# A two-layer decoder trunk on one core: where x's first pairs lie, when constants and late weights come, and which queue stores the solved triangle

## The chip, the core and the metric

The kernel runs on one core of a Trainium2 chip. The core has a matmul engine (TensorE, here PE, with its weight loads PEld), a vector engine (VectorE, DVE), a scalar engine (ScalarE, ACT), GpSimd (POOL) and SyncE (SP), which mostly issues transfers. SP, ACT and POOL issue DMAs, each in the order of its own queue. The metric is the device time of one execution in microseconds (us); the median of several runs is compared. The profiler records one execution.

## The reference

Two residual layers over 512 tokens of width 2048, all float32. Layer 0 is gated differential attention with 8 heads, layer 1 is RWKV-7 time mixing with 32 heads of 64 channels:

```python
x = x + diff_attention_mixer(rms_norm(x, norm_w[0]), ...)   # 8 heads, q k v gate = h @ w_in
x = x + rwkv7_mixer(rms_norm(x, norm_w[1]), ...)            # 32 heads

# attention, for each head
a = softmax(q1 k1) - lam * softmax(q2 k2)                    # causal
o = rms_norm(a @ v) * silu(gate)                             # then @ w_out

# RWKV, for each head and token t
sa = einsum('bhvk,bhk->bhv', S, a_t)
S = S * w_t + sa * b_t + v_t * k_t
y = einsum('bhvk,bhk->bhv', S, r_t)                          # then group norm, gate, @ w_out
```

## The kernel before, in words

**Products.** Each float32 product is made of three matmuls of rounded parts: a high part (`hH`, `wh`, made by ACT) and a low part (`hL`, `wl`, made by DVE as the difference, L105 and L106). Weights come in pieces of 512 KB into three buffers `wraw`, mostly on SP's queue (L78).

**Order of the queues.** The kernel is traced in Python, and an engine's queue is put in order from the tracing order, priorities (`high_priority(offset)`, with `AHEAD, SCAN, SOLVE = 2000, 3000, 4000`; a higher one goes first among what is expected to be ready) and `issue_after(ins)`, which puts an instruction behind `ins`. Beside the large products run *chains*: generators that are stepped by a count of matmuls. `tick` (L152) counts one matmul for the first chain in the list; a `yield n` in a generator waits for n matmuls. A chain that stands behind another in the list starts to count when that one is through.

**First layer.** `layer0` goes through the heads. Head 0 is made directly (`unit_tok`). Heads 1 to 7 (`unit_head`) use a block scheme in which sums of blocks of x are multiplied by sums of weight blocks: products with the sums S1, S2, S4 and S3 in turn, with products of plain blocks around them. A head has 336 matmuls on which chains are counted. The pairs of rows of x (`pairs`, eight tiles of two rows each) lie in tiles that later have another use: in order V, VL, acc1, G, Ta, Tb, Tc, Td. V and VL later hold a head's values (`head_vg`), acc1 and G the results of its value and gate products and the gate (`gates`, `copy_out`, L248). `input_sums` forms the sums from the pairs; S3, which goes into the places of x's first rows (`hH`, `hL`), is formed in a second call, `late`, once head 0's products have read these. Its high part is one ACT instruction (L491), its low part one on DVE (L492).

While the products of head h run, the attention of head h-1 is worked off as a chain (delay 56 matmuls, in head 1 20). In head 1 the chain `rwkv_consts` stands ahead of it: three DMAs on ACT's queue and some twenty small DVE operations (from L1161 on) that prepare parameters of the second layer, with 10 + 8 matmuls between its steps. In a head, `G` is needed by the products' copies (L248) once the attention of the head before has used its gate (L382); DVE's `take` (L527) then subtracts the product from G and acc1, and `third` writes the next products into the same accumulating bank. The last head works in another order: `square` comes before `third`, which loads its weights itself.

**Second layer.** `layer1` iterates 16 times over pairs of heads. An iteration makes the Gram products (`gram`, L1287, bank gp), stores parts of them on SP (`ltd`, L1301 and L1307), and POOL loads them back as LT. `t_solve` solves a triangular system on DVE in 31 small double steps (L1352, L1354), ends with a product into `Tm` (L1355) and stores it to HBM (`td`, L1356, on POOL's queue, 128 KB). `t_combine`, the first part of the scan's chain in the next iteration, reads it back in another arrangement (`TT`, four DMAs on SP, L1369), transposes two halves on DVE (L1378), waits `GAP_D` = 18 matmuls, makes the products `px` (L1384), and goes on after `GAP_X` = 19 and `GAP_T` = 8 more. Just behind px stand the next Gram products on PE, which need `AR` (L1271), formed on DVE from `mixr` (L1129). SP's queue holds, beside `td`'s readback, the loads of the weights.

Of the kernel before, what the change touches and what calls it, by code (L numbers as in the profile page):

```python
# [38 lines left out]
AHEAD, SCAN, SOLVE = 2000, 3000, 4000  # L39
# [423 lines left out]
NH4 = 8  # L463
# [3 lines left out]
def input_sums(g, pairs, late):  # L467


    nc, w = g.nc, g.work  # L470
    if not late:
        def parts(*tags):

            out, tags = [], list(tags)
            while tags:
                t = tags.pop(0)
                if t[:2] == "dd":
                    at = [g.const.tile([P, 2, 256], F32R, name="sum" + n, tag=n, bufs=1) for n in (t, tags.pop(0))]
                else:
                    at = w.tile([P, 2, 4, 256], F32R, name=t, tag=t, bufs=1)  # L480
                    at = [at[:, 0], at[:, 1]]
                out += [(at[0][:, k], at[1][:, k]) for k in range(at[0].shape[1])]
            return out

        g.sums = {"S1": parts("sA", "sA2"), "S2": parts("sB", "sB2"),
                  "S4": parts("dd0H", "dd0L", "dd1H", "dd1L", "sC2"),
                  "S3": [(g.hH[k][:, 256:512], g.hL[k][:, 256:512]) for k in range(NH4)]}

    def put(nm, k, o, scale=1.0):
        hi, lo = g.sums[nm][k]  # L490
        nc.scalar.activation(hi, o, AF.Copy, scale=scale)  # L491
        nc.vector.scalar_tensor_tensor(lo, o, scale, hi.bitcast(F32), ALU.mult, ALU.subtract)  # L492

    def mixed(o, x, scale, op):

        nc.vector.scalar_tensor_tensor(o, x, scale, o, ALU.mult, op)

    norm = lambda i: g.prm_a[:, i : i + 1]
    if not late:
        minus = g.const.tile([P, NH4], F32, name="minus")  # L500
        nc.vector.tensor_scalar(minus[:], g.prm_a[:, 0:NH4], -1.0, None, ALU.mult)
    for k in range(NH4):
        (a, b), (c, d) = [(pairs[k][:, i, 0:256], pairs[k][:, i, 256:512]) for i in range(2)]
        if late:
            put("S3", k, a, norm(k))
            continue
        nc.vector.tensor_scalar(d, d, norm(k + NH4), None, ALU.mult)
        mixed(d, b, norm(k), ALU.subtract)
        put("S1", k, d)
        mixed(d, a, minus[:, k : k + 1], ALU.add)  # L510
        put("S2", k, d)
        nc.vector.scalar_tensor_tensor(c, c, norm(k + NH4), d, ALU.mult, ALU.add)
        put("S4", k, c)
        nc.vector.tensor_sub(a, a, b)
# [15 lines left out]
def unit_head(g, aps, h, t1s, sq, turned):  # L530


    nc = g.nc
    c1, c2 = qk_cols(aps, h), vg_cols(aps, h)
    acc1 = g.work.tile([P, 2, 512], F32, name="acc1", tag="acc1", bufs=1)
    acc = [None, None, acc1[:, 0], acc1[:, 1]]
    q = [t[:] for t in t1s]
    N = NH4 // KG
    last = h == NH - 1

    def pair():
        return [g.pp.tile([P, 512], F32, name="pp", tag="pp") for _ in range(2)]

    def load(i, k0, parts):
        pool, tag, bufs = (g.work, "Te", 1) if i == N - 1 else (g.wraw, "wraw", 3)
        raw = pool.tile([P, KG, 512], F32, name="wraw", tag=tag, bufs=bufs)
        load_w(g, raw, parts, k0 + i * KG, slice(0, KG))
        return raw

    def split(raw):  # L550
        return split_w(g, None, KG, 512, 0, raw)

    def block(k0, t0):
        return lambda k, t: [x[k0 + k][:, t0 + t * P : t0 + (t + 1) * P] for x in (g.hH, g.hL)]

    def form(nm, i):
        return lambda k, t: [x[:, t * P : (t + 1) * P] for x in g.sums[nm][i * KG + k]]

    def products(out, lhs, raw, start=False, end=False):
        wt = split(raw)  # L560
        for t in range(2):
            first = start
            for lo in range(2):
                for k in range(KG):
                    for x in lhs(k, t)[: 2 - lo]:
                        m = nc.tensor.matmul(out[t][:], x, wt[lo][:, k, :], start=first, stop=end and lo == 1 and k == KG - 1,  # L566
                                             skip_group_check=True)
                        tick(g, m)
                        first = False

    def all_groups(out, lhs, raw, start=False, end=False, then=None):
        for i in range(N):
            r = raw(i)
            products(out, lhs(i), r, start and i == 0, end and i == N - 1)
            if then:
                add_w(g, r, then[0], then[1] + i * KG)

    def s4(out, keep, start=False, end=False):
        def raw(i):
            keep.append(load(i, NH4, c2))  # L580
            return keep[-1]
        all_groups(out, lambda i: form("S4", i), raw, start, end, None if last else (c2, 0))

    chained = lambda i: g.Ts[i]
    y = pair()
    all_groups(y, lambda i: block(NH4 + i * KG, 0), lambda i: load(i, NH4, c1), True, True)
    copy_out(g, q[:2], y)
    y = pair()
    all_groups(y, lambda i: block(i * KG, 0), chained, True, False, (c2, 0))
    take(g, q[:2], y)  # L590
    X = pair()
    all_groups(X, lambda i: form("S1", i), chained, True, last, (c2, NH4))
    copy_out(g, acc[2:], X)
    b22 = []
    if not last:
        s4(X, b22, end=True)
        G, acc[:2] = gates(g)
        copy_out(g, acc[:2], X)
    all_groups(y, lambda i: form("S2", i), chained, then=(c1, NH4))
    if last:  # L600
        G, acc[:2] = gates(g)
    take(g, acc[:2], y, ALU.subtract, acc[2:] if last else None)

    def square():
        X = pair()
        all_groups(X, lambda i: block(NH4 + i * KG, 256), chained, True, True)
        return X

    def third():
        for i in range(N):  # L610
            if last:
                b22.append(load(i, NH4, c2))
                add_w(g, b22[i], c2, i * KG)
            products(y, form("S3", i), b22[i], end=i == N - 1)
        take(g, acc[2:], y, ALU.subtract)

    head_qk(g, t1s, sq, [0, 1])
    if last:
        copy_out(g, q[2:], square())
        third()  # L620
        take(g, q[2:], y)
        head_qk(g, t1s, sq, [2, 3])
        turned()
        X = pair()
        s4(X, [], True, True)
        take(g, acc[:2], X)
        return head_vg(g, h, acc, G)
    turned()
    third()
    copy_out(g, q[2:], y)  # L630
    values = head_vg(g, h, acc, G)
    X = square()
    first_tiles(g, aps, h + 1)
    take(g, q[2:], X)
    head_qk(g, t1s, sq, [2, 3])
    return values
# [156 lines left out]
def layer0(g, aps):  # L793
    nc, tc = g.nc, g.tc
    lx = ExitStack()
    g.lc = lx.enter_context(tc.tile_pool(name="lc0", bufs=1))
    with ExitStack() as cx:
# [1 line left out]
        t1_tile = lambda: g.work.tile([P, 512], F32, name="t1", tag="t1", bufs=4)  # L799

        pairs = [g.work.tile([P, 2, T], F32, name="pair", tag=tag, bufs=1)
                 for tag in ("V", "VL", "acc1", "G", "Ta", "Tb", "Tc", "Td")]
        xT = [p[:, i] for i in range(2) for p in pairs]
        ss = g.const.tile([P, NT], F32, name="ss0")

# [83 lines left out]
        for h in range(NH):  # L889
# [15 lines left out]
            else:  # L905
# [5 lines left out]
                acc1 = g.work.tile([P, 2, 512], F32, name="acc1", tag="acc1", bufs=1)  # L911
                G, vg = gates(g)
# [5 lines left out]
                first_tiles(g, aps, 1)  # L918
                values = head_vg(g, h, vg, G)
            before = qkT + (sq,) + values  # L920
            if h == 0:
                Chain(g, rwkv_consts(g, aps))
                g.chains[0].step(g)
        rows = []
# [57 lines left out]
        def banks(i):  # L982
            if i < 2:
# [4 lines left out]
        load = loader(g, aps["da_w_out"], ((g.wraw, "wraw", 3), (g.work, "V", 1), (g.wraw, "wraw", 3),  # L988
                                              (g.work, "G", 1), (g.wraw, "wraw", 3)))
# [342 lines left out]
def t_solve(g, j, p):  # L1332


    nc, w = g.nc, g.work
    NQ = HALF // NG
    LT = w.tile([P, HALF + 1, HALF], F32, name="LT", tag="LT", bufs=1)
    Tm = w.tile([P, NQ, HALF], F32, name="Tm", tag="Tm", bufs=1)
# [14 lines left out]
                                       Tm[:, 0:s, i : i + 1].to_broadcast([P, s, n]), ALU.mult, ALU.mult)  # L1353
        nc.vector.tensor_add(Tm[:, 0:s, i + 1 :], Tm[:, 0:s, i + 1 :], tt)  # L1354
    nc.vector.tensor_mul(Tm[:], Tm[:], n2[:, None, :].to_broadcast([P, NQ, HALF]))  # L1355
    nc.gpsimd.dma_start(out=g.td[j % 2].rearrange("q l t -> l q t"), in_=Tm[:])  # L1356
    return ld.ins


GAP_D, GAP_X, GAP_T = 18, 19, 8  # L1360


def t_combine(g, j, p):

    nc, w, TT = g.nc, g.work, g.TT[j % 2]
    for h in range(2):
        for half in range(2):
            o, l0 = half * HALF, half * 16 + h * NC_
            nc.sync.dma_start(  # L1369
                out=TT[h * C + o : h * C + o + HALF, :, h, o : o + HALF],  # L1370
                in_=g.td[j % 2].rearrange("q (g l) t -> (q g) l t", g=NG)[:, l0 : l0 + NC_, :])
    T1 = w.tile([P, NC_, HALF], F32, name="T1", tag="T1", bufs=1)
    X = w.tile([P, NC_, HALF], F32, name="X", tag="X", bufs=1)
    px = g.ps.tile([P, 512], F32, name="px", tag="pd", bufs=1)
    for h in range(2):
        r_ = slice(h * C, h * C + C)
        with g.tc.issue_after(g.centred) if g.centred else ExitStack():
            nc.vector.transpose(T1[r_], TT[r_, :, h, 0:HALF])  # L1378
    yield GAP_D
    N = NC_ * HALF  # L1380
    blocks = [(h, h * C, slice(h * C, h * C + HALF), slice(h * C + HALF, h * C + C)) for h in range(2)]
    for h, b0, lo, hi in blocks:
# [373 lines left out]
```

## Time and profile before

| | |
|---|---|
| median of 3 runs | 2154.38 us (2148.98 to 2154.91) |
| the profiled execution | 2153.4 us, its span 2151.7 us |
| mean granted clock of PE | 0.987 |
| PE busy | 2105.0 us, 98% of the span |
| DVE busy | 1612.5 us, 75% |
| ACT busy | 1154.1 us, 54% |
| POOL busy | 389.8 us, 18% |
| DMA | 294.60 MB, mean 137 GB/s |

A row of the timeline or of the chain that ended last has its start and its length in us, then engine, line, operation, output<-inputs and the number of instructions merged (x), and in brackets the idle time of that engine before it and what ended it. A row of the waits reads "engine, line <- what it waited for: us in total, times, longest". A row of the windows gives a stretch's bounds and length, each engine's busy time with its instructions, then PEclk, the granted clock of PE (1.00 is full speed), the busy share of the DMA engines and the GB/s moved. SPq, POOLq and ACTq are DMA issues on these engines' queues; DMA rows of the chain run from the end of waiting to issue to the landing.

### The profile page before, as it was taken

How to read it: one execution, taken by the hardware profiler on the slowest of the kernel's cores; microseconds unless marked ns; L12 is line 12 of the kernel's file. 1: busy time of each engine (PE TensorE's matmuls, PEld its weight loads, DVE VectorE, ACT ScalarE, POOL GpSimd, SP SyncE). 2: the span in 40 equal slices, each digit the busy share in tenths (PEclk: the TensorE clock that was granted, in tenths of full speed). 3: DMA queues.
4: the chain of work that ended last, by engine and by line, in shares of the span. 5: the costliest groups of instructions: out<-in, count | busy, mean ns of one | idle time of the engine just before them, and what ended most of it. 6: DMA issues, size and time to landing. Idle time of an engine off the chain costs nothing.

```text
span 2151.7 us, 34077 instructions
## 1 busy us (share of the span) xinstructions
PE 2105.0 (98%) x11852; PEld 1708.5 (79%) x11852; DVE 1612.5 (75%) x4129; ACT 1154.1 (54%) x2278; POOL 389.8 (18%) x751
## 2 busy tenths in 40 slices
PE   9999999999999999999999999999999999999999
PEld 7788888888887788878677787787777778777887
DVE  6878988889887885667677777777767778767645
ACT  5665666566665543455455655556555555545322
POOL 1011211201113000101232222122222122221001
PEclk9999999999999999999899999999999999999999
DMA  8387978879789836623222332222323223346555
GB/s 263 121 179 191 176 173 186 165 189 178 170 187 215 292 118 186 140 80 104 68 80 76 94 94 86 81 91 75 101 84 94 84 91 91 94 130 190 178 164 121
DMA packets 143100, 294.60 MB, mean 137 GB/s; under 512 B 47968, under 2 KB 65376, under 8 KB 142928
## 3 DMA queue, kind: packets, MB, share of 16 engines
q1 hardware_dynamic: 93056, 180.72, 27.0%
q0 software_dynamic: 25216, 87.74, 22.2%
q10 hardware_dynamic: 24656, 23.97, 3.3%
q8 instruction: 93, 1.52, 0.3%
q14 instruction: 79, 0.65, 0.1%
HBM read 268.71 MB, written 23.66 MB: 136 GB/s over the span
## 4 chain that ended last, share of the span: by engine, by line
PE 71%; DVE 15%; DMA 7%; ACT 3%; issue 3%; POOL 0%; ACTq 0%; SPq 0%; POOLq 0%; DVEq 0%
PE pp L122 31%; PE pp L566 20%; PE pt L122 5%; DVE wl L106 4%; DMA td<-Tm 3%; PE gp L1287 2%; DMA TT<-td 1%; DVE tmpl L1352 1%; PE sm L1465 1%; PE sm L1483 1%; PE sc L122 1%; PE o L122 1%; PE sm L1476 1%; ACT wh L105 1%; PE lora L122 1%
## 5 line engine op out<-in xcount | busy, mean ns | idle before, releaser
L105 ACT CAST wh<-wraw 128x1024 fp32r<-128x1024 f32 (+2 forms) x291 | 303.6, 1043 | 343.4 <-PE pp L122 183.3
L106 DVE TENSOR_TENSOR wl<-wraw,wh 128x1024 fp32r<-128x1024 f32 (+2 forms) x291 | 358.1, 1231 | 142.6 <-ACT wh L105 126.1
L122 PE MATMUL pp<-hL,wh 128*128 128x512 f32 x1024 | 416.8, 407 | 0.0
L122 PE MATMUL pp<-hH,wl 128*128 128x512 f32 x1024 | 415.9, 406 | 0.3 <-DVE wl L106 0.3
L122 PE MATMUL pp<-hH,wh 128*128 128x512 f32 x1024 | 413.6, 404 | 0.0
L122 PEld LDWEIGHTS pp<-hH,wh 128*128 128x128 f32 x1024 | 195.0, 190 | 36.9 <-issue 2.4
L122 PEld LDWEIGHTS pp<-hL,wh 128*128 128x128 f32 x1024 | 195.0, 190 | 35.0
L122 PEld LDWEIGHTS pp<-hH,wl 128*128 128x128 f32 x1024 | 194.9, 190 | 33.4 <-DVE wl L106 0.7
L566 PE MATMUL pp<-wh,hH 128*128 128x512 f32 x448 | 178.4, 398 | 5.0 <-ACT acc L248 4.9
L566 PE MATMUL pp<-wh,hL 128*128 128x512 f32 x448 | 176.9, 395 | 0.0
L122 PE MATMUL pp<-wh,hH 128*128 128x512 f32 x372 | 145.8, 392 | 3.0 <-ACT hH L1088 3.0
L122 PE MATMUL pp<-wl,hH 128*128 128x512 f32 x372 | 145.9, 392 | 0.4 <-DVE wl L106 0.4
L122 PE MATMUL pp<-wh,hL 128*128 128x512 f32 x372 | 146.0, 392 | 0.2
L1352 DVE SCALAR_TENSOR_TENSOR tmpl<-LT,Tm 128x60 f32<-128x60 f32 (+24 forms) x496 | 135.2, 273 | 11.6
L566 PE MATMUL pp<-wl,hH 128*128 128x512 f32 x448 | 141.5, 394 | 0.4 <-DVE wl L106 0.4
L1471 POOL COPY SA<-VS 64x64 f32<-64x64 f32 x224 | 55.8, 249 | 469.4 <-DVE VS L1487 361.2
L1354 DVE TENSOR_TENSOR Tm<-Tm,tmpl 128x60 f32<-128x60 f32 (+24 forms) x496 | 104.3, 210 | 9.8
L566 PEld LDWEIGHTS pp<-wh,hH 128*128 128x128 f32 x448 | 85.0, 190 | 23.1 <-ACT acc L248 5.3
L566 PEld LDWEIGHTS pp<-wl,hH 128*128 128x128 f32 x448 | 85.0, 190 | 18.1 <-DVE wl L106 0.8
L566 PEld LDWEIGHTS pp<-wh,hL 128*128 128x128 f32 x448 | 85.0, 190 | 16.6
L1468 ACT COPY rhs<-sm 64x64 f32<-64x64 f32 x256 | 52.8, 206 | 74.4 <-PE sm L1465 72.2
L1478 ACT COPY VS<-sm 64x64 f32<-64x64 f32 x256 | 52.9, 207 | 59.8 <-PE sm L1476 55.0
(394 smaller groups left out, 4489.2 us busy)
## 6 DMA issues: line engine op xcount, KB each, us to landing
wraw<-in_rw_w_in_dram SPq DMA_DIRECT2D x128, 512.0 KB
wraw<-in_da_w_in_dram SPq DMA_DIRECT2D x75, 512.0 KB
wraw<-in_da_w_in_dram POOLq DMA_DIRECT2D x28, 512.0 KB, 6.6
wraw<-in_da_w_out_dram SPq DMA_DIRECT2D x26, 512.0 KB
wraw<-in_rw_w_out_dram SPq DMA_DIRECT2D x26, 512.0 KB
Ta<-in_da_w_in_dram POOLq DMA_DIRECT2D x21, 512.0 KB, 5.9
Tb<-in_da_w_in_dram POOLq DMA_DIRECT2D x21, 512.0 KB, 5.9
Tc<-in_da_w_in_dram POOLq DMA_DIRECT2D x21, 512.0 KB, 5.8
```

Source lines behind the costliest of these rows:

```text
L105: a = nc.scalar.copy(hi[:, ks], raw[:, ks])
L106: d = nc.vector.tensor_sub(lo[:, ks], raw[:, ks], hi[:, ks].bitcast(F32))
L122: m = nc.tensor.matmul(out, a, b, start=s, stop=e, skip_group_check=skip)
L566: m = nc.tensor.matmul(out[t][:], x, wt[lo][:, k, :], start=first, stop=end and lo == 1 and k == KG - 1, skip_group_check=True)
L1287: m = nc.tensor.matmul(gp[h][:, i * P : (i + 1) * P], BK[r_, c0 + i, :, :], p.AR[r_, c0 + i, :, :], start=True, stop=True)
L1352: nc.vector.scalar_tensor_tensor(tt, LT[:, i : i + 1, i + 1 :].to_broadcast([P, s, n]), n2[:, i : i + 1], Tm[:, 0:s, i : i + 1].to_broadca ...
L1354: nc.vector.tensor_add(Tm[:, 0:s, i + 1 :], Tm[:, 0:s, i + 1 :], tt)
L1465: nc.tensor.matmul(sm[:, 0:P], both(p.G[:, c, 0]), both(VS[:, c]), start=True, stop=True)
L1468: nc.scalar.copy(rhs[r_, :], sm[r_, h * C : h * C + C])
L1471: nc.gpsimd.tensor_copy(p.SA[r_, c - 1, :], VS[r_, c, h, :])
L1476: nc.tensor.matmul(sm[:, P : P + C], both(g.TT[j % 2][:, c]), rhs[:], start=True, stop=True)
L1478: nc.scalar.copy(VS[r_, c, h, :], sm[r_, P : P + C])
```

## The change

The edits, in the order of the diff:

- In `input_sums`, S3 of the first two pairs is formed at priority SCAN; the other six as before.
- In `unit_head`, the last head's four weight loads in `third` are put `issue_after` the last matmul of the S2 products.
- The eight tiles of x's pairs are named in another order: the first two pairs lie in acc1 and G, the third and fourth in V and VL.
- `rwkv_consts` is put in the list of chains at the end of head 1 instead of head 0; it stands ahead of the attention of head 1, in head 2.
- `t_solve` stores T by SP's queue instead of POOL's.
- `t_combine` waits 10 matmuls, traces the two transposes, waits 8 more and makes px: the 18 matmuls ahead of px are kept.

```diff
@@ input_sums
         if late:
-            put("S3", k, a, norm(k))
+            with g.tc.high_priority(offset=SCAN if k < 2 else 0):
+                put("S3", k, a, norm(k))
             continue
@@ unit_head
     all_groups(y, lambda i: form("S2", i), chained, then=(c1, NH4))
+    behind = g.m.ins
     if last:
...
             if last:
-                b22.append(load(i, NH4, c2))
+                with g.tc.issue_after(behind):
+                    b22.append(load(i, NH4, c2))
                 add_w(g, b22[i], c2, i * KG)
@@ layer0
         pairs = [g.work.tile([P, 2, T], F32, name="pair", tag=tag, bufs=1)
-                 for tag in ("V", "VL", "acc1", "G", "Ta", "Tb", "Tc", "Td")]
+                 for tag in ("acc1", "G", "V", "VL", "Ta", "Tb", "Tc", "Td")]
...
             before = qkT + (sq,) + values
-            if h == 0:
+            if h == 1:
                 Chain(g, rwkv_consts(g, aps))
                 g.chains[0].step(g)
@@ t_solve
-    nc.gpsimd.dma_start(out=g.td[j % 2].rearrange("q l t -> l q t"), in_=Tm[:])
+    nc.sync.dma_start(out=g.td[j % 2].rearrange("q l t -> l q t"), in_=Tm[:])
@@ t_combine
+    yield GAP_D - GAP_T
     for h in range(2):
         r_ = slice(h * C, h * C + C)
         with g.tc.issue_after(g.centred) if g.centred else ExitStack():
             nc.vector.transpose(T1[r_], TT[r_, :, h, 0:HALF])
-    yield GAP_D
+    yield GAP_T
```

## The prediction

> **What bounds the kernel now.** I read the page's busy times and the clock, then the waits of the matmul engine, the windows of low clock, and the timeline around each place that the change touches.
>
> ```profile
> PE 2105.0 (98%) x11852; PEld 1708.5 (79%) x11852; DVE 1612.5 (75%) x4129; ACT 1154.1 (54%) x2278; POOL 389.8 (18%) x751
> core 0: 2151.7 us, clock 0.987
> ```
>
> PE is busy for 98% of the 2151.7 us span. What is to be had without taking away products is its idle time (47 us) and the clock it lost, (1 - 0.987) x 2151.7 = 28 us of work. PE's waits name the idle time (us in total, times, longest):
>
> ```profile
> PE gp L1287 <- DVE AR L1271: 9.8, 12, 0.8
> PE px L1384 <- DVE T L1378: 5.3, 9, 1.0
> PE pp L566 <- ACT acc L248: 4.9, 1, 4.9
> PE px L1384 <- DVE y L1408: 3.8, 1, 3.8
> ```
>
> The first two come back in each iteration of the second layer, the third is one hole between heads 0 and 1 of the first layer, the fourth is in the second layer's first iteration. The windows show what follows such holes (after the times: length, then PE, PEld, DVE, ACT and POOL busy, PEclk, DMA share, GB/s):
>
> ```profile
> 104.40:111.20 6.80, 6.25 (x15) 4.90 (x16) 4.52 (x12) 6.69 (x16) 0.00 (x0) 0.50 0.86 281
> 1032.80:1046.40 13.60, 12.95 (x87) 10.10 (x88) 2.96 (x7) 4.87 (x10) 2.79 (x5) 0.50 0.45 122
> ...
> 1899.80:1903.20 3.40, 3.40 (x42) 3.18 (x39) 0.17 (x1) 1.71 (x5) 0.00 (x0) 0.50 0.59 195
> sum 54.50, PE 52.93 PEld 44.39 DVE 11.40 ACT 31.25 POOL 8.12; mean PE 5.88 PEld 4.93 DVE 1.27 ACT 3.47 POOL 0.90
> ```
>
> These are the first two and the last of nine windows at a clock of 0.50, 54.5 us in all, whose half, 27.2 us, accounts for the 28. The first follows the head hole and costs 3.4, the second the px wait of 3.8 and costs 6.8; the other seven (54.5 - 6.8 - 13.6 = 34.1 us) follow px and gp waits in the second layer and cost 17. So a hole costs its length, and often 1.7 or 3.4 us more behind it.
>
> **S3 early, x's first pairs in acc1 and G.** The hole, with two rows that group the S3 sums (duration in ns, then first and last start):
>
> ```profile
> 95.42 1.22 DVE L106 TENSOR_TENSOR wl<-wraw,wh 128x1024 fp32r<-128x1024 f32 x1
> ...
> 97.16 0.17 DVE L1161 TENSOR_SCALAR prm_hw<-pb 128x16 f32<-128x16 f32 x1
> ...
> 99.20 0.17 DVE L1168 COPY prm_bk_b<-prm_hkk 64x16 f32<-64x16 f32 x1
> ...
> 99.42 0.39 PE L122 MATMUL pp<-wl,hH 128*128 128x512 f32 x1
> ...
> 99.65 0.39 PE L122 MATMUL pp<-wh,hL 128*128 128x512 f32 x1
> ...
> 104.27 0.48 DVE L492 SCALAR_TENSOR_TENSOR hL<-pair,norms,hH 128x256 fp32r<-128x256 f32 x1
> 104.31 0.59 ACT L248 COPY acc<-pp 128x512 f32<-128x512 f32 x1 [1.98 <-DVE hL L492]
> ...
> 104.95 0.80 PE L566 MATMUL pp<-wh,hH 128*128 128x512 f32 x1 [4.92 <-ACT acc L248]
> L491 ACT ACTIVATE hH<-pair,norms x8: 492/494/508, 74.4 to 101.8; 128x256 fp32r<-128x256 f32 x8
> L492 DVE SCALAR_TENSOR_TENSOR hL<-pair,norms,hH x8: 476/478/480, 95.0 to 105.9; 128x256 fp32r<-128x256 f32 x8
> ```
>
> PE's last product of head 0 starts at 99.65, its next at 104.95. It needs banks that ACT frees by copying into acc1 and G, and those hold pairs 2 and 3 of x until DVE has made the low parts of their S3. ACT made the first high parts at 74.4; DVE began the low ones at 95.0, last in its queue, with the constants (97.16 to 99.37, 2.2 us) among them. After the change acc1 and G hold pairs 0 and 1, whose S3 has the scan's priority: two puts of 0.48 us on DVE, possible soon after 74.4, hidden under the products that run until 99.65. Pairs 2 and 3 lie in V and VL, which are written only after those copies, for an attention in the next head. The constants leave this stretch too. So 5.3 us from start to start shrink to a product's usual 0.23 (99.42 to 99.65): -5.1. Next late would be head 1's first weights, whose low part (wl) ends at 96.64, in time. Without the hole the 3.4 us of clock go: together **-8.5**. The lesser bound, a gain of 3.6, has 1.5 us of hole left by ACT's copies and the clock still halved.
>
> **Constants a head later.** In head 1 the attention of head 0 starts 18 matmuls earlier; PE has no long wait there: 0. In head 2 the constants' 18 steps now stand ahead of the attention of head 1, 18 x 0.23 = 4.1 us. What that meets:
>
> ```profile
> 260.29 0.48 DVE L382 SCALAR_TENSOR_TENSOR y<-o,ro,G 128x256 f32<-128x256 f32 x1
> 260.80 1.07 ACT L248 COPY G<-pp 128x512 f32<-128x512 f32 x2
> 261.84 0.68 DVE L527 TENSOR_TENSOR G<-G,pp 128x512 f32<-128x512 f32 x1
> 262.89 0.39 PE L566 MATMUL pp<-wh,hH 128*128 128x512 f32 x1
> ```
>
> The last y of the head before releases G, ACT copies into it, DVE subtracts (done at 262.52), and `third` may write its bank, at 262.89: 0.37 us of slack. With y 4.1 later PE waits 3.7, once; less if the attention, waiting on DVE and ACT as much as on its steps, catches up. The constants' 2.2 us of DVE are within it, and their DMAs go out long before use. Bounds 0 and 3.7, plus up to 3.4 of clock; I take **+2.5**, nearer the row's 3.7 than 0. The Trainium skill ("TensorE: Matmul & The Clock Gate", HAM oscillation) has only idle gaps over about 3.4 us re-throttle; by that 2.5 costs no clock. The trace disagrees: the 0.50 windows of the second layer follow waits of 1 us and less.
>
> **Late loads of the last head.** `issue_after` orders instructions of one engine's queue; a load on SP isn't held by the matmul it names. So **0**. If it did hold them, `square`, 48 products and 11 us, lies between that matmul and `third`: also 0.
>
> **T stored by SP, transposes traced later.** One iteration, and stores from issue to landing in the chain that ended last:
>
> ```profile
> 1505.82 2.33 SPq L78 DMA_DIRECT2D wraw<-in_rw_w_in_dram  x2
> ...
> 1507.89 0.42 DVE L1355 TENSOR_TENSOR Tm<-Tm,LT 128x256 f32<-128x256 f32 x1
> 1508.87 0.99 POOL L1356 DMA_DIRECT2D td<-Tm  x1 [4.84 <-DVE Tm L1355]
> ...
> 1513.45 1.82 SPq L1369 DMA_DIRECT2D TT<-td  x4
> ...
> 1515.27 0.44 DVE L1378 STREAM_TRANSPOSE T<-TT 64x256 f32<-64x256 f32 x1 [4.40 <-DMA TT<-td]
> 1515.63 1.18 DVE L106 TENSOR_TENSOR wl<-wraw,wh 128x1024 fp32r<-128x1024 f32 x1
> 1516.84 0.35 SPq L78 DMA_DIRECT2D wraw<-in_rw_w_in_dram  x1
> 1516.84 0.44 DVE L1378 STREAM_TRANSPOSE T<-TT 64x256 f32<-64x256 f32 x1
> ...
> 1518.10 0.69 DVE L1271 TENSOR_TENSOR AR<-mixr,E 128x512 f32<-128x512 f32 x1
> ...
> 1518.85 1.83 PE L1287 MATMUL gp<-AR,BK 64*128 64x128 f32 x28 [0.82 <-DVE AR L1271]
> 983.52 3.34 DMA ltd<-G
> 1508.87 4.51 DMA td<-Tm
> 1887.98 4.98 DMA td<-Tm
> 1508.00:1512.50 4.50, 4.50 (x57) 3.73 (x54) 1.99 (x7) 0.27 (x1) 1.29 (x3) 1.00 0.61 206
> 108.00:110.00 2.00, 2.00 (x6) 1.52 (x6) 1.97 (x5) 1.89 (x5) 0.00 (x0) 0.50 0.96 360
> ```
>
> T is ready at 1508.31, POOL issues 0.56 later, the store lands after 4.51, SP reads back at 1513.45, DVE (idle for 4.40) transposes at 1515.27; wl, the second transpose, mixr and AR stand behind it on DVE, so gp starts 0.82 late. All of it slides with the landing, until PE isn't held: by the waits 9.8 / 12 + 5.3 / 9 = 1.4 us per iteration.
>
> The trace has no such store from SP. The nearest row is SP's other small store, 3.34: **1.2 less** than 4.51, the good end. Against it, SP has just issued two loads of 512 KB, and its store goes behind them where POOL's goes beside. In the 4.5 us of POOL's store 206 GB/s were moved, 0.93 MB, of which the store is 0.13: 0.8 MB of loads were still ahead. At the 360 GB/s of a busy window they take 2.2 us, and 2.2 + 3.34 = 5.5 is **1.0 more**, the bad end, if nothing of the 3.34 overlaps. Most of it is the time before data flow and the receipt behind, so I take the middle, **0**. By the Trainium skill ("DMA: Bandwidth & Descriptors", Queues, rings and completion order) each DMA engine takes turns between queue rows packet by packet, and SP has one row, consumed in order; that speaks for the bad end, 5.5.
>
> Behind the store on SP's queue stand the readback, which needs it, and the next load, which waits for wl (1516.84) anyway: nothing. POOL loses the issues of 1 us each: 0, since nobody waits for what stands behind them. The transposes keep their priority, and px stays 18 steps on (10 + 8), so I leave DVE's order as it is: 0, with 0.5 more per iteration if both transposes go ahead of wl (the second's readbacks are issued 0.9 after the first's, DVE is busy for 0.44 of it), 1.4 less if both go behind AR. In the last two iterations the loads come after T is ready, so the store (4.98) would gain 1.6: PE's 1.1 and one window of 1.7, about **-2.5**, in the second last alone, as PE isn't held in the last.
>
> **Sum** against the profiled execution (span 2151.7, its time 2153.4): -8.5 + 2.5 + 0 - 2.5 = -8.5, 2144.9. The median of the three runs is 1.0 above it, so **2146**, own range 2140 to 2153.
>
> **The rivals.**
> 1. *Slower: the store is behind the loads* (or the second transpose ahead of wl). gp comes 0.5 to 1.0 later in 11 iterations, +5.5 to +11, and longer holes draw windows where there are none: 5 of 12 iterations, at 17 / 7 = 2.4 each, +12. With -6 from the first layer: +11.5 to +17, 2166 to 2171. It decides from about 0.3 us of delay, where the waits' gain in the first layer is used up. For: the 0.8 MB and the rule above. Against: POOL's 4.51 already contains the sharing.
> 2. *Much faster: the readback comes early, or the transposes go behind AR.* 15.1 us of waits and 17 of clock go: with -6, 2116; with half, 2132. For: 3.34, and DVE idling 4.40 with wl and mixr to do. Against: the loads.
> 3. *Head 2 takes it all back*: +3.7 and 3.4 against -8.5, and nothing in the second layer: -1.4, 2153.
> 4. *The hole stays*, since another S3 or copy ends last: -3.6 + 2.5 - 2.5, 2150.8; this and 3 are no change.
>
> **Chances.** The forecast 0.45, split at 0.3% (6.5 us, what a measurement of this kernel can tell): 0.29 faster, 0.16 same. Rival 1: 0.25. Rival 2: 0.20, faster. Rivals 3 and 4: 0.10, same. Faster 0.49, same 0.26, slower 0.25. The range that leaves out the outer half of rivals 1 and 2: 2124 to 2169.
>
> **What would show it.** Right: no wait `pp L566 <- ACT acc`, no 0.50 window near 105; hL's first starts near 75; a new wait of PE at about 260 behind G; td on SP, landing 4 to 5 us on, gp's wait near 9.8. Wrong: td landing after 5.5 and more windows (rival 1), or gp's and px's waits gone (rival 2); a wait of PE at 700 on loads (the late loads act).

## The result, and the profile after

The changed kernel takes 2131.97 us (median of 4, 2131.0 to 2134.03), the kernel before 2151.68 in the runs beside it (2146.9 to 2154.91): a ratio of 0.9911, 95% interval 0.9888 to 0.9935, or 14 to 24 us less. The forecast was 8.4 less. The kernel before spreads over more than 10 us from run to run, and over all its runs here its mean granted clock falls from 0.993 to 0.985 as the time grows, since its windows of low clock fall differently each time; so small differences below are read from the traces, not from the medians.

The page after, with the clock and the waits of PE (us in total, times, longest):

```profile
PE 2091.2 (98%) x11852; PEld 1690.3 (79%) x11852; DVE 1613.0 (76%) x4129; ACT 1155.5 (54%) x2278; POOL 367.9 (17%) x735
core 0: 2129.3 us, clock 0.996
PE sm L1480 <- ACT rhs L1472: 4.7, 12, 0.7
PE yt L391 <- DVE y L382: 3.9, 2, 3.4
PE px L1388 <- DVE T L1382: 3.3, 2, 3.2
PE gp L1290 <- DVE AR L1274: 0.7, 1, 0.7
```

`pp <- acc` (4.9) is gone, and gp's wait fell from 9.8 to 0.7. New are a wait of the scan (sm, 12 times) and one of 3.4 us in head 2. The windows that answer to those shown of before (length, then PE, PEld, DVE, ACT, POOL busy, PEclk, DMA share, GB/s):

```profile
97.00:105.00 8.00, 8.00 (x39) 6.58 (x38) 8.00 (x24) 7.57 (x15) 0.00 (x0) 1.00 0.91 314
257.80:264.60 6.80, 5.87 (x15) 4.40 (x16) 4.72 (x21) 3.97 (x10) 0.00 (x0) 0.50 0.33 108
1032.60:1042.90 10.30, 10.30 (x69) 7.81 (x68) 1.23 (x1) 3.81 (x10) 1.30 (x2) 0.50 0.45 134
1255.00:1899.00 644.00, 637.84 (x4399) 510.96 (x4399) 487.34 (x1340) 365.49 (x814) 150.15 (x368) 1.00 0.33 95
```

The hole between heads 0 and 1 and its window are gone (PE busy 8.00 of 8.00). A window of the same length has come in head 2, and the first iteration of the second layer still has one. In the steady iterations the clock is 1.00 throughout; before, seven windows lay there.

One steady iteration of the changed kernel, beside the one of before in the prediction:

```profile
1495.06 0.43 DVE L1358 TENSOR_TENSOR Tm<-Tm,LT 128x256 f32<-128x256 f32 x1
1495.56 0.38 SPq L1359 DMA_DIRECT2D td<-Tm  x1
...
1497.66 1.23 DVE L106 TENSOR_TENSOR wl<-wraw,wh 128x1024 fp32r<-128x1024 f32 x1 [2.18 <-ACT wh L105]
...
1498.48 1.83 SPq L1372 DMA_DIRECT2D TT<-td  x4
...
1499.70 0.69 DVE L1274 TENSOR_TENSOR AR<-mixr,E 128x512 f32<-128x512 f32 x1
...
1502.57 0.90 DVE L1382 STREAM_TRANSPOSE T<-TT 64x256 f32<-64x256 f32 x2
1503.02 2.06 PE L1290 MATMUL gp<-AR,BK 64*128 64x128 f32 x32
1505.00 1.09 PE L1388 MATMUL px<-T,G 32*32 32x32 f32 x32
```

Two orders differ from before. On DVE wl, mixr and AR now stand ahead of the transposes, so AR is ready 2.6 us before gp. On PE, px comes behind gp. The readback is issued 3.0 us after T is ready (1495.49), where it was 5.1.

The length of an iteration is read from gp's starts in the chain that ended last, eight iterations apart; first the kernel before, then the changed one:

```profile
1389.95 2.70 PE gp L1287 x32
1899.24 3.34 PE gp L1287 x32
```

```profile
1379.27 1.99 PE gp L1290 x32
1874.59 1.99 PE gp L1290 x32
```

Before 509.29 / 8 = 63.7 us, after 495.32 / 8 = 61.9: 1.75 less per iteration. The second layer gave nearly all of the result; the first layer must have given next to nothing.

### The profile page after: what moved, and what is told of

Same layout as the page of the kernel before. It is cut to its first block, busy times and chain, and to the rows that moved or that the text cites. A ratio compares the mean times of both kernels' runs of the same rounds, so it can differ in the third digit from the quotient of the medians.

```text
span 2129.3 us, 34082 instructions
## 1 busy us (share of the span) xinstructions
PE 2091.2 (98%) x11852; PEld 1690.3 (79%) x11852; DVE 1613.0 (76%) x4129; ACT 1155.5 (54%) x2278; POOL 367.9 (17%) x735
## 4 chain that ended last, share of the span: by engine, by line
PE 77%; DVE 10%; ACT 6%; issue 3%; DMA 3%; ACTq 0%; POOL 0%; SPq 0%; DVEq 0%; POOLq 0%
PE pp L122 36%; PE pp L567 21%; PE pt L122 4%; DVE wl L106 3%; ACT wh L105 1%; PE gp L1290 1%; PE sc L122 1%; PE sm L1480 1%; PE sm L1469 1%; PE sm L1487 1%; PE o L122 1%; DVE tmpl L1355 1%; ACT VS L1427 1%; PE lora L122 1%; PE z L122 1%
## 5 line engine op out<-in xcount | busy, mean ns | idle before, releaser
L567 PEld LDWEIGHTS pp<-wh,hH 128*128 128x128 f32 x448 | 84.7, 189 | 18.6 <-DVE G L528 1.2
L122 PEld LDWEIGHTS pp<-wh,hH 128*128 128x128 f32 x372 | 69.9, 188 | 19.6 <-ACT hH L1091 2.6
```

Source lines behind the costliest of these rows:

```text
L122: m = nc.tensor.matmul(out, a, b, start=s, stop=e, skip_group_check=skip)
```

## The experiments

Two theories for the second layer were set against each other: that the *queue* gained (a store from SP lands sooner), or that the *order* of DVE's and PE's queues, which comes out of the trace anew, gained. Each time below is a median, with that of the kernel before measured beside it.

**e1: the store alone.**

```diff
-    nc.gpsimd.dma_start(out=g.td[j % 2].rearrange("q l t -> l q t"), in_=Tm[:])
+    nc.sync.dma_start(out=g.td[j % 2].rearrange("q l t -> l q t"), in_=Tm[:])
```

> Kernel before with one edit: T stored by SP's queue; the transposes are traced where they were. Theory A (the order gained, not the queue): SP's store goes behind the two weight loads issued 2.5 and 0.5 us before T is ready and lands 4 to 5 us on, gp waits as before (9 to 10 us in all), the half-clock windows stay, 2150 to 2156 us. Theory B (the queue gained): the store lands after about 2 us as in the changed kernel, so the readback is there before mixr, gp's and px's waits (15 us) and most windows of the second layer go, and this edit alone gives nearly the whole gain, 2130 to 2137 us.

Measured: 2128.19 us (2124.97 to 2132.06), before 2146.53; ratio 0.993, 0.9903 to 0.9956. The time is even below theory B's range, but the landing is theory A's:

```profile
1494.08 2.33 SPq L78 DMA_DIRECT2D wraw<-in_rw_w_in_dram  x2
...
1496.15 0.43 DVE L1355 TENSOR_TENSOR Tm<-Tm,LT 128x256 f32<-128x256 f32 x1
1496.65 0.38 SPq L1356 DMA_DIRECT2D td<-Tm  x1
1501.42 1.82 SPq L1369 DMA_DIRECT2D TT<-td  x4
1501.58 1.22 DVE L106 TENSOR_TENSOR wl<-wraw,wh 128x1024 fp32r<-128x1024 f32 x1 [2.50 <-ACT wh L105]
1503.21 0.44 DVE L1378 STREAM_TRANSPOSE T<-TT 64x256 f32<-64x256 f32 x1 [0.41 <-DMA TT<-td]
...
1504.69 1.09 PE L1384 MATMUL px<-T,G 32*32 32x32 f32 x32
1504.79 0.69 DVE L1271 TENSOR_TENSOR AR<-mixr,E 128x512 f32<-128x512 f32 x1
...
1505.71 2.06 PE L1287 MATMUL gp<-AR,BK 64*128 64x128 f32 x32
```

The readback is issued 4.8 us after T is ready (1496.58), hardly sooner than before, and yet gp doesn't wait. The new thing is wl ahead of the first transpose: DVE does it while the readback is under way, and waits 0.41 where it waited 4.40. So neither theory as written: it looks as if the edit gained through an order that it changed on DVE. This trace alone doesn't show it, since the store moved with it; e9 below does.

**e2: the transposes alone traced later.**

```diff
+    yield GAP_D - GAP_T
     for h in range(2):
...
-    yield GAP_D
+    yield GAP_T
```

> Kernel before with one edit: the transposes traced 10 matmuls after the chain's start (10 + 8 in place of 18); the store stays on POOL. Theory A (the order gained): the Gram products' step of the chain now issues px behind gp where it issued the X products, DVE makes mixr and AR ahead of the transposes, gp doesn't wait, and this alone gives nearly the whole gain of the second layer, 2130 to 2136 us, with td still landing 4 to 5 us after its issue. Theory B (the queue gained): with the store at 4.5 us the transposes come late for px too, px waits instead of gp by about 1 us per iteration, 2145 to 2153 us.

Measured: 2136.38 us (2134.76 to 2139.26), before 2146.53; ratio 0.9954, 0.9939 to 0.9969. gp's wait is gone, as theory A has it, and an iteration takes what it takes in the changed kernel:

```profile
1385.41 1.99 PE gp L1287 x32
1880.75 1.99 PE gp L1287 x32
```

495.34 / 8 = 61.9 with the store on POOL. With e1 at 60.9 (below), this edit alone sets the changed kernel's iteration, and takes back about 1 us of what e1 gives. The landing came earlier here too, against what A expected: td on POOL was read back 2.85 us after its issue (1502.19 to 1505.04), where the two weight loads lay further ahead of it (5.1 and 2.3 us; in the kernel before 3.1 and 1.1).

**e3: the first layer's four edits.** `input_sums`, `pairs`, `rwkv_consts` and the last head's loads as in the change, the second layer as before.

> Kernel before with the first layer's four edits only. Theory A (gain given back): the hole between heads 0 and 1 and its window go (-8), head 2 gets a wait of 3.5 to 4.5 us behind G and a window of 3.4 (+8): 2149 to 2155 us, the same as before. Theory B (as forecast): -8.5 and +2.5, about 6 less than before, 2145 to 2148 us.

Measured: 2146.11 us (2139.73 to 2156.49), before 2146.53; ratio 1.0007, 0.9983 to 1.0031. In us the median lies in theory B's range, but the kernel before ran as fast beside it, and the interval, 3.6 us less to 6.7 more, leaves out B's gain of 6. Theory A: most of the hole's gain is given back, with the wait in the next head:

```profile
PE yt L391 <- DVE y L382: 3.9, 2, 3.4
```

The first gp, where the second layer's iterations begin, starts at 975.2 here and at 976.5 in the kernel before: 1.2 us less, not 6.

**e4: the constants back in head 1**, all else as in the change (`if h == 0:`).

> Changed kernel with one edit undone: the constants' chain stands in head 1 again, as before. Theory A: S3's priority and the places of the pairs alone close the hole between heads 0 and 1, and head 2's wait for G and its window go: about 8 us less than the changed kernel, 2122 to 2126 us. Theory B: the constants' 2.2 us on DVE ahead of the copies reopen part of the hole (2 us or more, with its window), and the gain is 3 us or less: 2128 to 2132 us.

Measured: 2123.9 us (2122.56 to 2132.37), before 2146.53; ratio 0.9911, 0.988 to 0.9943; the span is 2122.8 against 2129.3 of the changed kernel. The hole stays closed without moving the constants, and head 2's wait goes: theory A, with 6.5 us by the spans and 8 by the medians. Of the 6.5, the first layer has 4.3 (the first gp starts at 970.2 in place of 974.5); most of the rest is a shorter window of low clock (3.4 for 10.3) in the second layer's first iteration.

**e5: the store on SP, and the first transpose put ahead of wl again.**

```diff
+            held = g.hold.pop(0) if getattr(g, "hold", None) else None
+            if held:
+                after.enter_context(g.tc.issue_after(held))
             a = nc.scalar.copy(hi[:, ks], raw[:, ks])
...
-            nc.vector.transpose(T1[r_], TT[r_, :, h, 0:HALF])
+            t = nc.vector.transpose(T1[r_], TT[r_, :, h, 0:HALF])
+        if h == 0:
+            g.hold = [None, t.ins]
```

> Kernel of the run e1 (store on SP, nothing else) with DVE's order put back: the wl that e1 has ahead of the first transpose is traced issue_after that transpose, so DVE again stands before the readback with wl behind it. Theory A (DVE's order made e1's gain): td and its readback come as in e1, about 5 us after T is ready, but gp's waits are back (8 to 10 us in all), with windows of low clock behind them, 2141 to 2150 us. Theory B (the queue made it): the place of wl doesn't matter, as in e1, 2125 to 2132 us.

Measured: 2143.17 us (2138.65 to 2152.54), before 2146.92; ratio 0.9982, 0.9965 to 1.0. By the medians the gain is mostly gone, but this experiment is not clean: mixr came between the transpose and wl, so px waited (8.1 us in 11 times) instead of gp, in the first iteration the held wl made a hole of its own (PE waited 4.4 us on wl there, and 3.9 more behind it), and the steady iterations, 61.8 us, still lie 1.9 below those of the kernel before. It doesn't settle the case.

**e9: the store on POOL, DVE's order alone changed.** The reverse of e5, from iteration 4 on; `g.mixed` is the last DVE instruction of `shift_mix`.

```diff
-        with g.tc.issue_after(g.centred) if g.centred else ExitStack():
+        with g.tc.issue_after(g.centred) if g.centred else ExitStack(), \
+                g.tc.issue_after(g.mixed) if 4 <= j < D // P - 1 else ExitStack():
             nc.vector.transpose(T1[r_], TT[r_, :, h, 0:HALF])
```

> Kernel before with DVE's order alone changed: from iteration 4 on the two transposes are traced issue_after mixr, so wl and mixr go ahead of them; the store stays on POOL and nothing is moved on PE or SP. Theory A (DVE's order is the cause): td is read back about 5 us after T is ready as before, yet DVE uses that time for wl, the transposes start no later, gp's waits fall from 9.8 to under 2 us, and the windows behind them go: 61 us per iteration as in e1, 2125 to 2133 us. Theory B (the queue is the cause): gp and px wait as before, 63 us per iteration, 2141 to 2151 us.

Measured: 2123.24 us (2121.68 to 2125.54), before 2147.61; ratio 0.9886, 0.986 to 0.9911. Theory A, and a little below its range:

```profile
1495.61 0.42 DVE L1355 TENSOR_TENSOR Tm<-Tm,LT 128x256 f32<-128x256 f32 x1
1496.59 0.99 POOL L1356 DMA_DIRECT2D td<-Tm  x1 [4.84 <-DVE Tm L1355]
1500.66 1.82 SPq L1369 DMA_DIRECT2D TT<-td  x4
1501.05 1.23 DVE L106 TENSOR_TENSOR wl<-wraw,wh 128x1024 fp32r<-128x1024 f32 x1 [2.45 <-ACT wh L105]
...
1502.85 0.43 DVE L1379 STREAM_TRANSPOSE T<-TT 64x256 f32<-64x256 f32 x1
...
1503.94 0.69 DVE L1271 TENSOR_TENSOR AR<-mixr,E 128x512 f32<-128x512 f32 x1
...
1505.18 2.06 PE L1287 MATMUL gp<-AR,BK 64*128 64x128 f32 x32
DVE T L1379 <- DMA TT<-td: 16.9, 19, 4.3
```

The last row in the kernel before:

```profile
DVE T L1378 <- DMA TT<-td: 58.6, 17, 6.1
```

The queues of PE, POOL and SP have the same instructions in the same order as before, and so has ACT's but for one pair of neighbours; on DVE only wl and mixr have moved, in eleven iterations. The readback is issued 4.6 us after T is ready. DVE's waits for it fell from 58.6 us to 16.9, and gp starts 9.1 us after T is ready where it started 10.5 after. The length of an iteration in e1 and in this kernel:

```profile
1384.19 2.06 PE gp L1287 x32
1871.19 1.99 PE gp L1287 x32
```

```profile
1383.64 1.99 PE gp L1287 x32
1871.20 2.06 PE gp L1287 x32
```

487.00 / 8 = 60.9 and 487.56 / 8 = 60.9: the order alone gives all that e1 gave, and more than the change. The 2.7 us per iteration, like the change's 1.75, is counted against one trace of before, with 63.7; the traces of e3, e7 and e8, whose second layer is that of before, have 62.9 to 64.1, so it is 2.0 to 3.2.

**e7 and e8: the hole's two edits apart**, the priority and the places, one run each.

> Kernel before with S3 of the first two pairs at the scan's priority, which pairs still lie in V and VL. Theory: the hole stays, since acc1 and G hold pairs 2 and 3, whose S3 keeps its place: a wait of 4 to 5 us of pp on acc near 100 us, 2140 to 2150 us. Rival: priority alone makes room on DVE and the hole falls below 3 us.

> Kernel before with the first two pairs in acc1 and G, no priority. Theory: DVE makes the low parts of these two at 95.0 as it did, first of the eight, before the last product at 99.65: the hole closes by the places alone, no wait over 1 us there, 2133 to 2141 us. Rival: without the priority they still come behind 99 us, and 2 us or more of hole are left.

Measured: e7 2142.61 us, e8 2150.54 us, above its expected range; a single run doesn't tell either from before. Their traces do:

```profile
PE pp L567 <- ACT acc L248: 1.9, 1, 1.9
```

That is e7: with the priority alone 1.9 of the 4.9 us remain, and no window follows; the expected 4 to 5 was wrong, the rival right. In e8 PE has no wait there: the places alone close the hole, though DVE begins the low parts at 96.2, later than before.

**e6, e10, e11: versions that beat both kernels.** All have the places and the priority, constants in head 1, the transposes' trace and the yields of before. e6 adds the store on SP, e10 the order of e9 with the store on POOL, e11 both.

> Kernel before with three edits: the store on SP, the first two pairs in acc1 and G, their S3 at the scan's priority. Constants in head 1 and transposes where they were. Theory: e1's second layer (61.0 us per iteration, where the changed kernel has 61.9) and the first layer without its hole and window (8 less): 2117 to 2122 us, faster than the changed kernel by 10 or more. Rival: the hole's 8 us are hidden in the noise of windows elsewhere and the result is e1's, 2125 to 2130 us.

> Kernel e9 with the first two pairs in acc1 and G and their S3 at the scan's priority; the store on POOL. Theory A: the same as e6, 2116 to 2124 us, a little over it, since SP's store shortens the first iterations' px wait too. Theory B: 8 us less than before at most, 2134 to 2143 us.

> Kernel e10 (DVE's order set, S3 and places) with the store on SP in place of POOL: DVE's order is the same in both, so this is the queue by itself. Theory A: the store lands behind the same two weight loads on either queue, nothing waits for it now: 2115 to 2119 us as e10's 2117.1. Theory B: SP's store lands earlier where no load is ahead, in the first and the last two iterations, and 3 us or more are gained: 2110 to 2114 us.

Measured: e6 2121.18 us (2116.32 to 2123.1), ratio to before 0.9884, 0.9859 to 0.9909; e10 **2117.1** us (2115.35 to 2118.32), 0.9858, 0.9829 to 0.9887; e11 2121.95 us (2119.54 to 2125.96), 0.9885, 0.986 to 0.991. e10, with the store where it was, is the fastest kernel of this study, about 15 us below the changed one by the medians, 11 by the ratios to before. e11 against e10 moves the store alone, but on PE, DVE and ACT the orders of the first iterations changed with it; it is the queue by itself in the steady ones only. There it makes no difference (61.0 and 60.9 us per iteration). The whole is 5 us longer in these runs, which neither theory expected, though the intervals overlap. By the traces, one early iteration is 5.5 us longer, with a window of low clock, and the stretch behind the last gp 3.7, among it the last readback. The chain's rows of e10 and, second, of e11:

```profile
1913.52 3.40 DMA TT<-td
```

```profile
1917.29 6.58 DMA TT<-td
```

In e11 wl stands behind that readback on DVE, PE waits 3.1 us for it, and a window of low clock follows. Why this readback takes longer stays open.

## Why the prediction was right or wrong

**The hole (-8.5).** Right. pp's wait on acc and the window went; PE runs through at a clock of 1.00. In e6 and e10, which have these two edits and no other in the first layer, the first gp starts 7.7 and 9.2 us earlier than in the kernel before. e7 and e8 show that the places carry it, and that the priority alone would have left 1.9 us.

**The constants (+2.5).** The mechanism was right, the size too small, and what rival 3 has for head 2 came true:

```profile
257.40 0.48 DVE L382 SCALAR_TENSOR_TENSOR y<-o,ro,G 128x256 f32<-128x256 f32 x1
257.92 1.07 ACT L248 COPY G<-pp 128x512 f32<-128x512 f32 x2 [2.81 <-DVE y L382]
257.94 0.69 PE L391 MATMUL yt<-ident,y 128*128 128x128 f32 x2 [3.44 <-DVE y L382]
258.68 1.28 DVE L528 TENSOR_TENSOR G<-G,pp 128x512 f32<-128x512 f32 x2
259.42 0.79 PE L567 MATMUL pp<-wh,hH 128*128 128x512 f32 x1 [0.79 <-DVE G L528]
```

PE waits 3.44 and 0.79, 4.2 us together, against the bound of 3.7, and a window of 6.8 at half the clock follows, which costs 3.4: 7.6. The attention did not catch up; all of its 18 steps came through, and 0.5 us more. The forecast took a middle between the ends where the row of 0.37 us of slack left no reason for one. By the Trainium skill ("TensorE: Matmul & The Clock Gate", HAM oscillation) the rule is no idle gaps of PE over about 3.4 us. The wait of 3.44 us was followed by a window, as by that rule; the windows after px's and gp's waits of 1 us and less in the kernel before are not explained by it.

**The late loads (0).** Right: e4 has this edit and e6 has not, and in their traces the first layer has the same instructions in the same order on every queue.

**The store on SP (0).** Right for this edit alone: 4.8 us in e1 from issue to readback, against 4.6 after POOL's issue in the kernel before (1508.87 to 1513.45). In the changed kernel it was wrong: 2.9 (1495.56 to 1498.48), below even the good end of 3.34. The sum took the two loads to stand just ahead of the store; with the transposes' edit they lay 4.6 and 1.8 us ahead. POOL's store sped up likewise in e2, so the loads ahead matter to it on either queue. The Trainium skill's rule ("DMA: Bandwidth & Descriptors", Queues, rings and completion order), by which SP's row goes in order, spoke for the bad end, 5.5; e1 has 4.8 there, with the two loads just ahead.

**"I leave DVE's order as it is: 0."** This is the step that failed. The prediction named both other orders, 0.5 more and 1.4 less, and the DVE idle time of 4.40 with wl and mixr to do, and then took neither. The queues' order is made anew at each trace from what is expected to be ready. With the store alone on SP (e1), wl was put ahead of the transposes; with the transposes' edit (e2, and the changed kernel) wl, mixr and AR were, and gp's wait went from 9.8 us to 0.7. e9 shows that such an order is enough, with the store where it was: 24 us less.

**"px stays 18 steps on (10 + 8)."** Also wrong. The chain counts matmuls only while it is first in the list, and `gram` steps it once by itself. Before, px came by the count, ahead of gp, and that step issued the X products, just behind gp. With one more yield it issues px, behind gp, and the X products come 19 matmuls later. So the scan runs later, and an iteration takes 61.9 us where the store's edit alone gives 60.9. The windows of eight iterations, the changed kernel and then e1 (length, then PE, PEld, DVE, ACT, POOL busy, PEclk, DMA share, GB/s):

```profile
1379.20:1874.52 495.32, 490.42 (x3362) 392.88 (x3361) 378.26 (x1039) 279.98 (x623) 112.43 (x280) 1.00 0.32 92
1384.19:1871.12 486.93, 485.04 (x3361) 394.79 (x3361) 378.99 (x1040) 277.79 (x624) 120.93 (x280) 1.00 0.32 95
```

PE idles 4.9 us against 1.9, mostly in the scan's products (sm on rhs), which is 3.0 of the 8.4 us; the other 5.4 appear as busy time of PE, with the small products at other places among the large ones. What makes them longer there stays open.

**The sum.** The first layer's terms are -8.5 + 7.6 = -0.9. The chain's rows of the first gp, before and after, have -2.0 there:

```profile
976.51 1.99 PE gp L1287 x32
```

```profile
974.55 1.99 PE gp L1290 x32
1922.35 8.44 DMA td<-Tm
```

The last gp starts at 1899.24 and at 1874.59, 24.7 earlier: 22.7 more in the second layer, of which the last eight iterations are 14.0, the first iteration's shorter window (10.3 for 13.6) some 1.7, and the iterations between the rest. From there to the end 2.3 are given back, since the spans differ by 22.4.

The prediction's -2.5 was for the second last iteration, and there it had the right way: the store is read back 3.2 us after its issue in place of 5.0, and the last gp follows the one before it after 62.0 us in place of 65.2, 1.5 more than the steady iterations gain. What is given back lies in the last iteration, which the prediction put at nothing since PE isn't held there: the last store, on SP, took 8.44 us to land in place of 4.97 (1946.78 in the kernel before), with loads beside it, and PE waited 1.6 us before px for a `y` that DVE makes behind the late transposes. How much of this is the queue isn't shown, since e2 has 6.4 there from POOL.

Rival 2 (waits and windows gone, 2116 to 2132) was the case that came: its readback came early too, but the order is what e9 shows to suffice. The likeliest case, 2140 to 2153, missed the result; the range as a whole holds it only because it was drawn out to take in half of this rival. The rival's price was fair: 15.1 of waits and 17 of clock over 12 iterations are 2.7 each, and e9 gained as much against the same trace. Rival 1 did not come but for that last store.

## What to carry to other kernels

Where an engine idles in front of a transfer while work behind it in its queue is ready, that order is the thing to change: read what stands behind the waiting instruction before judging the transfer. In a kernel whose queues are ordered from the trace, a small edit to a DMA can gain through an order it upsets, so an experiment that forces the order by itself is worth more than one that moves the DMA. And a generator stepped from two places must be recounted when a yield is added.

## What the runs showed of the hardware

In head 2 a wait of 4.2 us cost 7.6, since a window of 6.8 us at a clock of 0.50 followed; in e3, with 4.4 us of waits at the same place, the window was 3.4. In the second layer of the kernel before, waits of 1 us and less were followed by such windows too, where PE had only small matmuls around them: with gp's and px's waits gone, one of the seven windows of the steady iterations is left in e1 and none in e9. The four runs of e10 lie within 3 us, where those of the kernel before lie over more than 10; but one run of e4, whose steady iterations have no such window in its trace, lies 8 us above its others.

A 128 KB store behind two 512 KB loads took as long from either queue: from T's end to the issue of the readback a median of 5.1 us in the steady iterations, both from POOL (before) and from SP (e1). With no load issued in the 5 us ahead of it, SP's was the shorter: 2.3 us in e1's second and third iterations, where it was 3.6 and 3.4 from POOL in the kernel before.
